# Decays folded into the queries of the linear attention, and the softmax attention's query preparation written behind its scores

## The chip, the cores and the metric

One NeuronCore of a Trainium2 chip runs the whole block as one program. The metric is the device time of one launch in microseconds (us), as the median of three runs. Matrix work is done by TensorE (PE in the profile; its weight loads are listed apart as PEld), elementwise work by VectorE (DVE) and ScalarE (ACT), a little by GpSimd (POOL). Transfers are issued by SyncE (SP).

## The reference

One encoder block over 1024 tokens of width 1024, all in float32. Two branches read the same normalised input; only what the change touches is spelled out here.

```
h = RMSNorm(x);  [linear q,k,v,r, gate codes, softmax q,k,v, branch gates] = h @ W_in
# linear attention, 4 heads, keys of 128, values of 256, forward and backward:
#   S_t = exp(log_g_t) * S_{t-1} + k_t v_t^T,   o_t = q_t^T S_t
q_dec = q * exp(b); k_inv = k * exp(-b)                 # b: running sum of log_g in a chunk
o = tril(q_dec k_inv^T) v  +  q_dec @ state             # state of the chunks before
state = exp(b_last) * state + k_tail^T v
# softmax attention, 8 query heads on 2 key heads, blocks of 128, window +-128, sink:
p = softmax([scores of three neighbouring key blocks, sink]);  o = p v
x = x + (sigmoid(gA) * (A @ W_a) + sigmoid(gB) * (B @ W_b)) @ W_out
x = x + SwiGLU(RMSNorm(x))
```

The decay `exp(b_last)` is one number for each key channel. It multiplies the state by rows, and the query meets the state along the same channels; so the decay may as well multiply the query.

## The kernel before, in words

Large products are computed as three matmuls on split operands: each float32 tensor becomes a rounded high part (ACT copies it to fp32r) and a low part (DVE subtracts). `wunit` (lines 66 to 73) loads a weight tile, splits it on ACT (line 70) and DVE (line 72), and the dense projections use it.

The program runs in stages: projections to DRAM scratch (to about 330 us), linear attention (about 330 to 545 us), softmax attention (about 545 to 735 us), output projections and the feed-forward part (to the end). In the two attention stages the dense projections that are still due fill TensorE: `slot(stages, n)` (line 206) calls the stage functions of one step in a given order and lets n matmuls of dense work run, spread evenly between them. TensorE takes its instructions in just this written order (`manual_schedule`). The other engines' queues are ordered by a list scheduler which prefers what is written earlier among what its model takes to be ready; so moving a function in the source moves its instructions on ACT, DVE and SP, and may move others too.

Linear attention works on 32 chunks of 128 tokens (4 heads by 8), two chunks (a pair) at a time for the gates. `g_gates` (625) computes the running sums `cs` and their small summary `sm`; `g_powers` (662) makes the powers, and from them `en` (keys) and `q2` (queries, forward and backward); `g_scores` (683) transposes keys and makes the masked scores; `g_out` (708) makes the key-value products `kv` of a chunk, carries the forward state `pf` and adds query times state to the output `o`; `g_back` (735) and `g_back_out` (747) do the same backwards with `kb`, `o2`; `g_turn` (767) transposes the output. In `g_out` ACT makes the decay `dec` (a [128,1] exponential, line 719), then the decayed state `th` (721), which TensorE multiplies by the queries; DVE makes the next state (722). `g_back` does likewise with `decb` (741), `thb` (743) and line 745. `k_norm` (780) normalises and rotates the softmax attention's keys, written at the stage's end, and the scheduler lets it float forward.

Softmax attention works on 16 steps (2 key heads by 8 blocks; 4 query heads at a time). `a_prep` (905) normalises and rotates queries on ACT (866) and DVE (912 to 917); `a_turn` (919) transposes them; `a_scores` (931) makes the scores of four heads, each in a PSUM bank, which DVE masks, copies out and reduces to a maximum (line 941); after the fourth, DVE makes the negative maximum `nm` (948 to 950), ACT takes four exponentials (956), DVE adds up (`dn`, 958) and inverts, GpSimd scales (962). `a_probs` (964) transposes probabilities two steps later, ACT and DVE split them (976, 977), and `a_out` (980) multiplies them with the values; ACT copies the result out (`sob`, 987). All these small products share four PSUM banks (`chtile`, line 49), while dense work has four of its own. Within a step the functions are sorted by the tuple `order`:

```
order = (a_probs, k_prep, a_prep, a_scores, a_turn, k_turn, a_out, k_load, a_load)
```

Of the kernel before, what the change touches and what calls it, by code (L numbers as in the profile page):

```python
# [11 lines left out]
AF = mybir.ActivationFunctionType  # L12
ALU = mybir.AluOpType

P = 128
# [15 lines left out]
def body(tc, i, out):  # L31
    nc = tc.nc
    with ExitStack() as root:
# [8 lines left out]
        def nm(s):  # L42
            uid[0] += 1
            return f"{s}_{uid[0]}"
# [4 lines left out]
        def chtile(shape, dt=F32):  # L49
            return psc.tile(list(shape), dt, tag="ch", name=nm("ch"))  # L50
# [24 lines left out]
        def mm(o, a, b, start, stop):  # L75
            nc.tensor.matmul(o, a, b, start=start, stop=stop)  # L76

        def mm3(o, ah, al, bh, bl, start, stop):
            mm(o, ah, bh, start, False)
            mm(o, ah, bl, False, False)  # L80
            mm(o, al, bh, False, stop)
# [459 lines left out]
        with tc.manual_schedule(engines={mybir.EngineType.PE}):  # L541
# [8 lines left out]
            for k in range(KT):  # L550
# [5 lines left out]
                c = slice((k % 4) * P, (k % 4 + 1) * P)  # L556
# [63 lines left out]
        def gtile(tag, shape=(P, 256), dt=F32, bufs=2):  # L620
            return gt.tile(list(shape), dt, tag=tag, name=nm(tag), bufs=bufs)

        gla = {}
# [38 lines left out]
        def g_powers(hd, c):  # L662

            pr = gla[hd, c].pr
            qk, e, cs = pr.qk, pr.e, pr.cs
            ef, csf = (v.rearrange("p d j t -> p (d j t)") for v in (e, cs))
            nc.vector.tensor_tensor(e[:, 0], cs[:, 0], cs[:, 0, :, 63:64].to_broadcast([P, 2, P]), op=ALU.subtract)
            nc.vector.tensor_tensor(e[:, 1, :, 1:P], cs[:, 1, :, 0:P - 1], cs[:, 1, :, 63:64].to_broadcast([P, 2, P - 1]),
                                    op=ALU.subtract)
            nc.vector.tensor_scalar(e[:, 1, :, 0:1], cs[:, 1, :, 63:64], -1.0, None, op0=ALU.mult)  # L670

            x1 = cs.rearrange("p d j t -> p d (j t)")
            x2 = e.rearrange("p d j t -> p d (j t)")
            nc.scalar.activation(csf, ef, AF.Exp, scale=-1.0 / 16)
            nc.scalar.activation(ef, ef, AF.Exp, scale=1.0 / 16)
            pr.en = gtile("en", (P, 2, 256))
            nc.vector.tensor_tensor(pr.en[:, 0], x2[:, 0], qk[:, 1], op=ALU.mult)
            nc.vector.tensor_tensor(pr.en[:, 1], x1[:, 1], qk[:, 1], op=ALU.mult)
            pr.q2 = (gtile("q2f", bufs=3), gtile(f"q2b{c}", bufs=(3, 2, 2, 1)[c // 2]))
            nc.vector.tensor_tensor(pr.q2[0], x1[:, 0], qk[:, 0], op=ALU.mult)  # L680
            nc.vector.tensor_tensor(pr.q2[1], x2[:, 1], qk[:, 0], op=ALU.mult)
# [26 lines left out]
        def g_out(hd, c):  # L708

            a = gla[hd, c]  # L710
            kv = chtile((P, 2, 256))
            for d in range(2):
                mm3(kv[:, d], a.kth[:, d], a.ktl[:, d], a.vh, a.vl, True, True)
            a.pf = gtile("pf")
            if c:
                pf = gla[hd, c - 1].pf
                dec = gtile("dec", (P, 1))
                p = gla[hd, c - 1]
                nc.scalar.activation(dec, a.pr.sm[:, 0, a.j, 0:1], AF.Exp, bias=p.pr.sm[:, 0, p.j, 1:2])
                th = gtile("th")  # L720
                nc.scalar.activation(th, pf, AF.Copy, scale=dec[:, 0:1])
                nc.vector.scalar_tensor_tensor(a.pf, pf, dec[:, 0:1], kv[:, 0], op0=ALU.mult, op1=ALU.add)
                a.kb = gtile(f"kb{c}", bufs=2 if c < 5 else 1)
                nc.scalar.copy(a.kb, kv[:, 1])
            else:
                nc.vector.tensor_copy(a.pf, kv[:, 0])
                a.kb = None
            o = chtile((P, 256))
            mm3(o, a.sh, a.sl, a.vh, a.vl, True, c == 0)
            if c:  # L730
                mm(o, a.pr.q2[0][:, a.t], th, False, True)
            a.ob = gtile(f"ob{c}", bufs=2 if c < 5 else 1)
            nc.scalar.copy(a.ob, o)

        def g_back(hd, c):

            a = gla[hd, c]
            if c < NC - 1:
                n = gla[hd, c + 1]
                dec = gtile("decb", (P, 1))  # L740
                nc.scalar.activation(dec, a.pr.sm[:, 1, a.j, 1:2], AF.Exp, bias=n.pr.sm[:, 1, n.j, 0:1])
                a.thb = gtile("thb")
                nc.scalar.activation(a.thb, n.kb, AF.Copy, scale=dec[:, 0:1])
                if c:
                    nc.vector.scalar_tensor_tensor(a.kb, n.kb, dec[:, 0:1], a.kb, op0=ALU.mult, op1=ALU.add)

        def g_back_out(hd, c):
            a = gla[hd, c]
            if c < NC - 1:
                o2 = chtile((P, 256))  # L750
                mm(o2, a.pr.q2[1][:, a.t], a.thb, True, True)
                nc.vector.tensor_tensor(a.ob, a.ob, o2, op=ALU.add)
            if c:
                g_back(hd, c - 1)

            if c % 2:
                a.ss = gtile("oss", (P, 2))
            ss = a.ss if c % 2 else gla[hd, c + 1].ss
            sq = gtile("osq", bufs=1)
            nc.scalar.activation(sq, a.ob, AF.Square, accum_out=ss[:, 1 - c % 2:2 - c % 2])  # L760
            if c % 2 == 0:
                rs = gtile("ors", (P, 2))
                rsqrt(rs, ss, 1.0 / 256, EPS, epst, gt, (P, 2), "on")
                for j, v in enumerate((gla[hd, c + 1].ob, a.ob)):
                    nc.scalar.activation(v, v, AF.Copy, scale=rs[:, j:j + 1])
# [41 lines left out]
        for n in range(NH * NC):  # L807
            hd, c = divmod(n, NC)
# [11 lines left out]
        with tc.manual_schedule(engines={mybir.EngineType.PE}):  # L820
            fill(24)
            for t in range(last + 1):
                n = 24 if t < 2 else 16 if t < 4 else 12 if t < NH * NC + 4 else 8 if t < last - 1 else 18
# [56 lines left out]
        def k_load(t):  # L880
            raws[t] = sw.tile([P, 256], F32, tag="kvr", name=nm("kvr"))
            need(("skv", t))
            nc.sync.dma_start(out=raws[t], in_=scr["skv", t][:, 256:512])
            keys[t] = sw.tile([P, 2, P], F32, tag="key", name=nm("key"))
            nc.sync.dma_start(out=keys[t].rearrange("p a b -> p (a b)"), in_=scr["key", t])
# [127 lines left out]
        for n in range(2 * KT):  # L1013
# [9 lines left out]
                if n:  # L1023
                    todo[n - 1].append((k_load, n))
            todo[n].append((a_load, g, t))
        order = (a_probs, k_prep, a_prep, a_scores, a_turn, k_turn, a_out, k_load, a_load)
        k_load(0)
        with tc.manual_schedule(engines={mybir.EngineType.PE}):
            for t, v in enumerate(todo):
# [507 lines left out]
```

## Time and profile before

| | |
|---|---|
| median of 3 runs | 1645.83 us (1645.22 to 1646.64) |
| the profiled execution | 1645.61 us, its span 1643.8 us |
| PE busy in the span | 1626.0 us, 99% |
| DVE, ACT, POOL busy | 1251.4, 842.6, 76.0 us |
| granted TensorE clock | 1.000 |
| transfers | 262.91 MB, 160 GB/s on average |

The profile is one execution; its rows of time (windows, waits, groups of equal instructions, timeline) count microseconds from the span's start. An engine's busy time holds the instructions themselves and not their waiting; matmuls overlap in their records, so PE looks busy as long as it is fed. A row of waits names who waited, at which line, for whom, the total, how often and the longest.

### The profile page before, as it was taken

Reading aid. Unit: us, or ns where it says so; the run is one execution under the profiler, and the core shown is the slowest. Engines: PE = TensorE matmul, PEld = TensorE weight load, DVE = VectorE, ACT = ScalarE, POOL = GpSimd, SP = SyncE. Lnnn points to the kernel's source line nnn. Section 1 sums busy time; section 2 is a strip of 40 time slices with the busy share of each in tenths; the row PEclk is TensorE's granted clock in tenths of the full one; section 3 lists DMA queues with packets and bytes.
Section 4 is the critical chain, followed back from the end, with each engine's and each line's share of the span. In section 5 each row is a group of like instructions: output and inputs, shape, how many; then the busy total and the mean of one; then the engine's idle time right before and its main releaser. Section 6 shows DMA issues by size and latency. Waiting matters only on the chain.

```text
span 1643.8 us, 23281 instructions
## 1 busy us (share of the span) xinstructions
PE 1626.0 (99%) x7588; PEld 1346.0 (82%) x7588; DVE 1251.4 (76%) x2559; ACT 842.6 (51%) x1762; POOL 76.0 (5%) x68
## 2 busy tenths in 40 slices
PE   9999999999999989999999999999999999999999
PEld 7888888888888778888888888888888888888887
DVE  8866665589986598867885678887777778779655
ACT  8622224468998666665554557333333333354442
POOL 0000000000000034540000000000000000000000
PEclk9999999999999999999999999999999999999999
DMA  7554334475554633248765544443334443596433
GB/s 238 176 178 148 115 122 135 173 250 173 179 161 129 191 108 97 77 138 280 225 205 175 168 146 145 140 149 109 109 115 147 142 147 129 177 341 193 149 98 119
DMA packets 168010, 262.91 MB, mean 160 GB/s; under 512 B 19324, under 2 KB 52860, under 8 KB 167888
## 3 DMA queue, kind: packets, MB, share of 16 engines
q1 hardware_dynamic: 167888, 261.42, 49.8%
q8 instruction: 60, 0.98, 0.2%
q14 instruction: 62, 0.51, 0.1%
HBM read 187.93 MB, written 73.42 MB: 159 GB/s over the span
## 4 chain that ended last, share of the span: by engine, by line
PE 84%; DVE 9%; ACT 4%; DMA 2%; issue 1%; POOL 1%; SPq 0%; ACTq 0%; DVEq 0%
PE mm L76 23%; PE mm L306 9%; PE mm L308 9%; PE mm L307 9%; PE mm L1350 7%; PE ch L1350 5%; PE ch L76 4%; PE ch L306 4%; PE ch L308 4%; PE ch L307 4%; PE ch L460 3%; PE mm L460 2%; ACT p L956 1%; DVE wl L72 1%; DVE cs L655 1%
## 5 line engine op out<-in xcount | busy, mean ns | idle before, releaser
L298 ACT ACTIVATE wh<-ws 128x512 fp32r<-128x512 f32 x132 | 83.3, 632 | 195.9 <-PE mm L307 102.2
L70 ACT ACTIVATE wh<-wr 128x512 fp32r<-128x512 f32 x202 | 124.9, 626 | 87.4 <-PE mm L76 54.9
L72 DVE TENSOR_TENSOR wl<-wr,wh 128x512 fp32r<-128x512 f32 x202 | 137.7, 686 | 26.8 <-ACT wh L70 26.4
L299 DVE TENSOR_TENSOR wl<-ws,wh 128x512 fp32r<-128x512 f32 x132 | 90.5, 686 | 22.7 <-ACT wh L298 22.6
L298 ACT ACTIVATE wh<-wr 128x512 fp32r<-128x512 f32 x69 | 43.6, 632 | 124.8 <-issue 49.7
L962 POOL TENSOR_SCALAR p<-p,rd 128x384 f32<-128x384 f32 (+1 forms) x64 | 75.8, 1202 | 657.1 <-DMA qr<-sq 587.2
L298 ACT ACTIVATE wh<-a 128x512 fp32r<-128x512 f32 x64 | 40.5, 633 | 91.4 <-PE ch L1350 42.3
L76 PE MATMUL mm<-wh,xl 128*128 128x512 f32 x192 | 83.1, 433 | 0.0
L76 PE MATMUL mm<-wh,xh 128*128 128x512 f32 x192 | 79.6, 415 | 0.0
L76 PE MATMUL mm<-wl,xh 128*128 128x512 f32 x192 | 79.6, 414 | 0.0
L299 DVE TENSOR_TENSOR wl<-a,wh 128x512 fp32r<-128x512 f32 x64 | 44.2, 691 | 43.1 <-ACT wh L298 42.5
L1350 PE MATMUL mm<-hh,wh 128*128 128x512 f32 x176 | 68.5, 389 | 0.0
L1350 PE MATMUL mm<-hl,wh 128*128 128x512 f32 x176 | 68.5, 389 | 0.0
L1350 PE MATMUL mm<-hh,wl 128*128 128x512 f32 x176 | 68.5, 389 | 0.0
L76 PE MATMUL mm<-xl,wh 128*128 128x512 f32 x160 | 64.5, 403 | 0.1
L76 PE MATMUL mm<-xh,wh 128*128 128x512 f32 x160 | 64.4, 403 | 0.2 <-ACT wh L70 0.2
L76 PE MATMUL mm<-xh,wl 128*128 128x512 f32 x160 | 59.2, 409 | 0.0
L1320 DVE TENSOR_TENSOR hl<-hr,hh 128x512 fp32r<-128x512 f32 x75 | 51.4, 685 | 3.7 <-ACT hh L1319 3.7
L1350 PE MATMUL ch<-hh,wh 128*128 128x512 f32 x132 | 51.3, 389 | 0.0
L1350 PE MATMUL ch<-hl,wh 128*128 128x512 f32 x132 | 51.3, 389 | 0.0
L1350 PE MATMUL ch<-hh,wl 128*128 128x512 f32 x132 | 51.3, 389 | 0.0
L76 PE MATMUL mm<-oah,wh 128*128 128x512 f32 x128 | 50.2, 392 | 0.0
(620 smaller groups left out, 5077.7 us busy)
## 6 DMA issues: line engine op xcount, KB each, us to landing
wr<-in_w_fi_dram SPq DMA_DIRECT2D x102, 256.0 KB
wr<-in_w_f_dram SPq DMA_DIRECT2D x80, 256.0 KB
wr<-in_w_t_dram SPq DMA_DIRECT2D x56, 256.0 KB
B<-c SPq DMA_DIRECT2D x44, 256.0 KB
T<-tx SPq DMA_DIRECT2D x44, 256.0 KB
a<-in_w_fo_dram SPq DMA_DIRECT2D x44, 256.0 KB
hr<-T SPq DMA_DIRECT2D x44, 256.0 KB
wr<-in_w_ob_dram SPq DMA_DIRECT2D x32, 256.0 KB
```

What stands on the lines that cost most here:

```text
L70: nc.scalar.activation(h, raw, AF.Copy)
L72: nc.vector.tensor_tensor(l, raw, h.bitcast(F32), op=ALU.subtract)
L76: nc.tensor.matmul(o, a, b, start=start, stop=stop)
L298: nc.scalar.activation(h, src, AF.Copy)
L299: nc.vector.tensor_tensor(l, src, h.bitcast(F32), op=ALU.subtract)
L306: nc.tensor.matmul(o, h[:, c], x[kk][0], start=start and kk == 0, stop=False, skip_group_check=True)
L307: nc.tensor.matmul(o, h[:, c], x[kk][1], start=False, stop=False, skip_group_check=True)
L308: nc.tensor.matmul(o, l[:, c], x[kk][0], start=False, stop=kk == nk - 1, skip_group_check=True)
L460: nc.tensor.matmul(ys[m], a[:, c], b, start=f0, stop=f1, skip_group_check=True)
L962: nc.gpsimd.tensor_scalar(p[:, h, :w], p[:, h, :w], rd[:, h:h + 1], None, op0=ALU.mult)
L1320: nc.vector.tensor_tensor(l, r, h.bitcast(F32), op=ALU.subtract)
L1350: nc.tensor.matmul(ys[m], a[:, c], b, start=f0, stop=f1, skip_group_check=True)
```

## The change

Two edits. First, in the linear attention, all decays of a pair of chunks are made at once: DVE adds the two log decays for each chunk boundary into a small tile `dec` ([128, 2, 2]), and ACT takes one exponential of it for the pair. The decay then multiplies the 128x128 slice of queries in place on DVE, and TensorE multiplies these queries by the undecayed state (`pf`, or the next chunk's `kb`). ACT no longer makes `th` and `thb`. The state updates on DVE stay, with the new decay as their scalar. Second, in the softmax attention, `a_scores` stands ahead of `k_prep` and `a_prep` in the step's order.

```diff
@@ g_powers
+            pr.dec = gtile("dec", (P, 2, 2), bufs=16)
+            nc.vector.tensor_tensor(pr.dec[:, 1], pr.sm[:, :, 1, 0], pr.sm[:, :, 0, 1], op=ALU.add)
+            if c:
+                nc.vector.tensor_tensor(pr.dec[:, 0], pr.sm[:, :, 0, 0], gla[hd, c - 1].pr.sm[:, :, 1, 1], op=ALU.add)
+            dc = pr.dec[:, 0 if c else 1:2]
+            nc.scalar.activation(dc, dc, AF.Exp)
@@ g_out
-                dec = gtile("dec", (P, 1))
-                p = gla[hd, c - 1]
-                nc.scalar.activation(dec, a.pr.sm[:, 0, a.j, 0:1], AF.Exp, bias=p.pr.sm[:, 0, p.j, 1:2])
-                th = gtile("th")
-                nc.scalar.activation(th, pf, AF.Copy, scale=dec[:, 0:1])
-                nc.vector.scalar_tensor_tensor(a.pf, pf, dec[:, 0:1], kv[:, 0], op0=ALU.mult, op1=ALU.add)
+                dec = a.pr.dec[:, a.j, 0:1]
+                q = a.pr.q2[0][:, a.t]
+                nc.vector.tensor_scalar(q, q, dec, None, op0=ALU.mult)
+                nc.vector.scalar_tensor_tensor(a.pf, pf, dec, kv[:, 0], op0=ALU.mult, op1=ALU.add)
...
-                mm(o, a.pr.q2[0][:, a.t], th, False, True)
+                mm(o, q, pf, False, True)
@@ g_back
-                dec = gtile("decb", (P, 1))
-                nc.scalar.activation(dec, a.pr.sm[:, 1, a.j, 1:2], AF.Exp, bias=n.pr.sm[:, 1, n.j, 0:1])
-                a.thb = gtile("thb")
-                nc.scalar.activation(a.thb, n.kb, AF.Copy, scale=dec[:, 0:1])
+                dec = (n if a.j else a).pr.dec[:, 1 - a.j, 1:2]
+                q = a.pr.q2[1][:, a.t]
+                nc.vector.tensor_scalar(q, q, dec, None, op0=ALU.mult)
+                a.after = n.kb
                 if c:
-                    nc.vector.scalar_tensor_tensor(a.kb, n.kb, dec[:, 0:1], a.kb, op0=ALU.mult, op1=ALU.add)
+                    nc.vector.scalar_tensor_tensor(a.kb, n.kb, dec, a.kb, op0=ALU.mult, op1=ALU.add)
@@ g_back_out
-                mm(o2, a.pr.q2[1][:, a.t], a.thb, True, True)
+                mm(o2, a.pr.q2[1][:, a.t], a.after, True, True)
@@
-        order = (a_probs, k_prep, a_prep, a_scores, a_turn, k_turn, a_out, k_load, a_load)
+        order = (a_probs, a_scores, k_prep, a_prep, a_turn, k_turn, a_out, k_load, a_load)
```

The numbers of instructions that change: ACT loses 28 `th`, 28 `thb` and 56 single decays and gains 16 exponentials of a pair; DVE gains 28 small additions and 56 multiplications of a query slice. TensorE has the same matmuls as before, in nearly the same places.

What this does to the engines' queues is seen at three places. The first is ACT in the linear attention, in the step after the transposed output of an earlier head, about the chunk whose state update is `pf_4541` before. `kb` and `ob` are the copies that free the two PSUM banks of `g_out`, `osq`, `oss` and `rl` belong to the output's normalisation, `kth` is the next chunk's split keys. Before:

```order
L741 ACTIVATE decb_4902<-sm_4026,sm_4197 128x1
L760 ACTIVATE osq_4519,oss_4406<-ob_751_3586 128x256
L98 ACTIVATE rl_4522<-oss_4406,eps 128x2
L99 ACTIVATE rl_4522<-rl_4522 128x2
L724 COPY kb_1055_4547<-ch_4534 128x256
L733 COPY ob_1057_4554<-ch_4549 128x256
L721 ACTIVATE th_4630<-pf_4541,dec_4628 128x256
L695 ACTIVATE kth_4565<-ch_4562 128x256
```

In the changed kernel the same place reads (its line numbers are 5 to 7 higher here, and `st` is dense work's output, `ob` with `ors` the normalisation's last step):

```order
L765 ACTIVATE osq_4501,oss_4391<-ob_750_3591 128x256
L98 ACTIVATE rl_4504<-oss_4391,eps 128x2
L99 ACTIVATE rl_4504<-rl_4504 128x2
L729 COPY kb_1028_4526<-ch_4516 128x256
L738 COPY ob_1030_4533<-ch_4528 128x256
L186 ACTIVATE st_4559<-mm_3976,rstdt 128x512
L770 ACTIVATE ob_771_3665<-ob_771_3665,ors_4503 128x256
L770 ACTIVATE ob_750_3591<-ob_750_3591,ors_4503 128x256
L702 ACTIVATE kth_4544<-ch_4541 128x256
```

The decayed state and the single decay are gone from between the bank-freeing copies, and other work stands closer behind them.

The second place is DVE in the second step of the softmax attention's scores. `dn` and `rd` belong to the first step's softmax, `st` and `wl` to dense work, `rt` to the queries' normalisation. Before, the four rows of line 941, which free the score banks, begin here:

```order
L914 TENSOR_TENSOR sq_7173<-qr_7166,qB 128x4x64
L125 TENSOR_TENSOR st_7193<-mm_6983,rstd 128x512
L917 TENSOR_TENSOR qn_7186<-qn_7186,sq_7173 128x512
L958 TENSOR_TENSOR dn_7130<-dn_7130,es_7127 128x4
L102 TENSOR_TENSOR rt_7181<-rt_7181,rl_7178 128x4
L125 TENSOR_TENSOR st_7197<-mm_6984,rstd 128x512
L960 RECIPROCAL rd_7136<-dn_7130 128x4
L103 SCALAR_TENSOR_TENSOR rt_7181<-rt_7181,rl_7178 128x4
L72 TENSOR_TENSOR wl_7206<-wr_7202,wh_7204 128x512
L104 SCALAR_TENSOR_TENSOR rs_7177<-rt_7181,rl_7178 128x4
L941 ISA p_7209,mx_7210<-ch_7211,band 128x384
```

In the changed kernel the rows of the same step (line 946 there) come like this:

```order
L932 TENSOR_TENSOR sql_7042<-ch_7036,sqh_7041 128x512
L908 TENSOR_TENSOR kTl<-ch_7046,kTh 128x2x128
L72 TENSOR_TENSOR wl_7090<-wr_7086,wh_7088 128x512
L946 ISA p_7062,mx_7063<-ch_7064,band 128x384
L946 ISA mx_7063 128x1
L125 TENSOR_TENSOR st_7077<-mm_6875,rstd 128x512
L963 TENSOR_TENSOR dn_6999<-dn_6999,es_6996 128x4
L946 ISA p_7062,mx_7063<-ch_7070,band 128x384
L946 ISA mx_7063 128x1
L965 RECIPROCAL rd_7005<-dn_6999 128x4
L125 TENSOR_TENSOR st_7081<-mm_6876,rstd 128x512
L946 ISA p_7062,mx_7063<-ch_7093,band 128x384
```

The first bank-freeing row has moved ahead of the first step's sum `dn` and of the dense work's two outputs, and the queries' preparation is no longer before it.

The third place is ACT in a middle step of the softmax attention. `sqh` splits the turned queries, `sob` copies the output of `a_out`, lines 956 and 961 are the exponentials, `ph` splits the turned probabilities of the next step. Before:

```order
L926 ACTIVATE sqh_7945<-ch_7940 128x512
L987 COPY sob_7961<-ch_7951 128x512
L953 ACTIVATE es_7924<-es_7924 128x4
L956 ACTIVATE p_7894,dn_7927<-p_7894,nm_7920,rs_7591 128x384 x4
L976 ACTIVATE ph_7977<-ch_7972 128x512
```

The same step in the changed kernel:

```order
L931 ACTIVATE sqh_7837<-ch_7832 128x512
L961 ACTIVATE p_7767,dn_7800<-p_7767,nm_7793,rs_7545 128x384
L958 ACTIVATE es_7797<-es_7797 128x4
L961 ACTIVATE p_7767,dn_7800<-p_7767,nm_7793,rs_7545 128x384 x3
L992 COPY sob_7853<-ch_7843 128x512
L981 ACTIVATE ph_7869<-ch_7864 128x512
```

The copy of the output has moved from ahead of the exponentials to behind them. It stands ahead of them in 10 of the 16 steps before and in 5 of the 16 in the changed kernel.

## The prediction

> **What bounds the kernel now.** I read the page's busy times first, then the table of windows by stage, then the waits of TensorE's weight loads in the two attention stages, and last the timeline at the places found.
>
> ```profile
> span 1643.8 us, 23281 instructions
> PE 1626.0 (99%) x7588; PEld 1346.0 (82%) x7588; DVE 1251.4 (76%) x2559; ACT 842.6 (51%) x1762; POOL 76.0 (5%) x68
> ```
>
> TensorE is busy in 99% of the span, so the total is its work plus 17.8 us of idleness. No change here removes TensorE work; what can be won is waiting. The windows (columns: stretch, its length, busy time and instructions of PE, PEld, DVE, ACT, POOL, then clock and transfers) say where that is. The first three are the linear attention, the next two the softmax attention.
>
> ```profile
> 345.00:385.00 40.00, 40.00 (x235) 34.85 (x234) 37.13 (x124) 31.15 (x81) 0.00 (x0) 1.00 0.67 204
> 385.00:465.00 80.00, 78.56 (x456) 66.00 (x455) 77.65 (x283) 73.62 (x225) 0.00 (x0) 1.00 0.57 174
> 465.00:545.00 80.00, 79.00 (x443) 66.58 (x442) 55.94 (x172) 70.67 (x215) 0.00 (x0) 1.00 0.47 141
> 545.00:605.00 60.00, 55.24 (x274) 44.68 (x272) 43.55 (x137) 36.74 (x99) 9.06 (x8) 1.00 0.54 165
> 605.00:735.00 130.00, 125.22 (x680) 105.36 (x681) 107.65 (x353) 86.17 (x227) 66.76 (x56) 1.00 0.31 98
> 735.00:1643.00 908.00, 905.09 (x3992) 748.15 (x3990) 692.49 (x1108) 392.18 (x661) 0.00 (x0) 1.00 0.51 165
> ```
>
> From 735 us on TensorE is busy 905.09 of 908.00 us, so a microsecond won earlier arrives at the end nearly whole. In the linear attention ACT is busy 92% from 385 to 465 us and DVE 97%, and TensorE begins to miss. In the softmax attention TensorE loses 4.76 and 4.78 us while no engine is full: there chains of latency decide. PE's idle time understates the loss, since the records of matmuls overlap; a weight load that stands still says it better. Its waits from 345 to 545 us:
>
> ```profile
> PEld ch L76 <- ACT ob L733: 3.5, 6, 0.9
> PEld ch L771 <- ACT ob L765: 1.3, 2, 0.9
> PEld ch L771 <- DVE ktl L696: 1.3, 2, 0.7
> PEld ch L76 <- DVE ktl L696: 1.3, 4, 0.5
> PEld ch L76 <- ACT kb L724: 1.1, 3, 0.5
> ```
>
> 5.9 us of waiting are ACT's (3.5 + 1.3 + 1.1), 2.6 us DVE's; 8.5 us together. From 545 to 735 us the longest are these, the last two rows being PE's own:
>
> ```profile
> PEld ch L76 <- DVE mx L941: 4.4, 5, 0.9
> PEld ch L923 <- DVE mx L941: 2.5, 2, 2.3
> PEld ch L76 <- DVE pl L977: 2.5, 4, 1.0
> PEld ch L973 <- POOL p L962: 1.8, 3, 0.8
> ...
> PE ch L923 <- DVE mx L941: 1.9, 1, 1.9
> PE ch L973 <- POOL p L962: 0.9, 2, 0.6
> ```
>
> Three of the four weight-load rows wait for DVE to free a bank of scores (941) or of turned probabilities (977).
>
> **The decays: what ACT loses.** The groups from 345 to 545 us:
>
> ```profile
> L721 ACT ACTIVATE th<-pf,dec 128x256 f32<-128x256 f32 x28 | 14.5, 518 | 0.2
> L743 ACT ACTIVATE thb<-kb,decb 128x256 f32<-128x256 f32 x28 | 14.1, 511 | 1.1 <-PE ch L76 1.1
> ...
> L741 ACT ACTIVATE decb<-sm 128x1 f32<-128x1 f32 x16 | 4.6, 286 | 0.8 <-DVE sm L660 0.7
> L719 ACT ACTIVATE dec<-sm 128x1 f32<-128x1 f32 x15 | 4.6, 304 | 0.0
> ```
>
> 14.5 and 14.1 us go with the decayed states. The 56 single exponentials go at between 0.286 and 0.304, say 0.295 us: 16.5 us. Sixteen exponentials of four numbers or fewer come back at the same price, 4.7 us. ACT is relieved of 14.5 + 14.1 + 16.5 - 4.7 = 40.4 us over 200 us, that is 16.2 us in an 80 us window: 73.62 falls to about 57, or 72%. At 345 to 385 us ACT was busy 31.15 of 40.00, 78%, and TensorE idle for nothing. So I expect most of ACT's 5.9 us of waits to go and take seven tenths: 4.1 us. Bounds: nothing, and all 5.9.
>
> **What DVE gains.** The prices come from these groups of the same window:
>
> ```profile
> L72 DVE TENSOR_TENSOR wl<-wr,wh 128x512 fp32r<-128x512 f32 x38 | 26.0, 687 | 5.0 <-ACT wh L70 5.0
> ...
> L705 DVE CAST sh<-sp 128x128 fp32r<-128x128 f32 x32 | 7.1, 223 | 0.2
> L650 DVE TENSOR_SCALAR e<-e 128x512 f32<-128x512 f32 x15 | 6.3, 423 | 0.4 <-ACT e L648 0.4
> L793 DVE SCALAR_TENSOR_TENSOR qn<-kvr,rs,kg 128x128 f32<-128x128 f32 x16 | 5.4, 348 | 0.2
> ...
> L659 DVE TENSOR_SCALAR sm<-cs 128x8 f32<-128x8 f32 x15 | 2.5, 166 | 0.0
> ```
>
> No row shows a 128x128 multiplication by a column of scalars. From below: 423 ns for 512 and 166 ns for 8 elements make 0.51 ns an element, so 166 + 61 = 227 ns for 128, near the cast's 223. From above: the operation with two tensors and such a scalar, 348 ns. I take 250, close to the cast, since it too has one source: 56 x 0.25 = 14.0 us (12.5 to 19.5). The 28 additions at the 128x8 row's 166 ns are 4.6 us. DVE gains 18.6 us (17.1 to 24.1), and its 170.7 us (37.13 + 77.65 + 55.94) become 189.3 of 200, or 95%. That was about its share at 345 to 385 us (37.13 of 40.00), where TensorE did not wait. In the queue the additional work stands where its data have long been there: the queries were last read by the scores two steps earlier, the decay by the pair's powers. Behind a multiplication stands the state's update, which waits for `kv` anyway. So the price is that `ktl` and the bank-freeing copies come a little later; I let DVE's 2.6 us of waits grow by half, 1.3 us. Linear attention: -4.1 + 1.3 = -2.8 us.
>
> A rule of the Trainium skill bears on the first price. Row L72, with two tensors, takes 687 ns for 512 elements, row L650, with one, 423. "VectorE: DVE Perf Modes", in the section on mode 2x_2P, says that a float32 operation with a single SBUF source streams two elements a cycle, and one with two tensors one, which these two rows agree with. Its 0.96 GHz would make 67 ns of the 128 elements, an estimate from that page, and the 56 multiplications about 12.5 us instead of 14.0.
>
> **The order of the scores.** TensorE's work is the same, with the dense matmuls around the scores shifted by two or three. What changes is when DVE frees score banks. At the stage's start:
>
> ```profile
> 586.24 0.16 DVE L958 TENSOR_TENSOR dn<-dn,es 128x4 f32<-128x4 f32 x1
> 587.98 0.55 DVE L941 CUSTOM_DVE_ANT_0 p<-ch,band 128x384 f32<-128x384 f32 x1
> 588.60 0.66 PE L923 MATMUL ch<-ident,qn 128*128 128x128 f32 x4 [1.86 <-DVE mx L941]
> ```
>
> The second step's first score bank was read at 587.98 us, 1.7 us after `dn`, and TensorE's transposes had stood for 1.86 us. In the changed queue that read stands ahead of `dn`, and the other three are only two larger rows behind it. So this 1.9 us should go, and with the earlier maximum the exponentials and GpSimd's scaling come earlier, for which the turned probabilities of the first two steps waited 0.9 us. I take 2.5 of these 2.8 us (bounds 0 and 2.8), since the next wait, for `sqh` or a bank of `pl`, is near.
>
> In the middle of the stage two effects oppose each other. ACT's queue there:
>
> ```profile
> 641.83 0.17 DVE L950 TENSOR_SCALAR nm<-mx 128x4 f32<-128x4 f32 x1
> 642.35 0.59 ACT L987 COPY sob<-ch 128x512 f32<-128x512 f32 x1 [1.96 <-PE ch L76]
> 642.94 0.70 ACT L956 ACTIVATE p<-p,nm,rs 128x384 f32<-128x384 f32 x1
> ACT sob L987 <- PE ch L76: 16.9, 10, 2.0
> ```
>
> The negative maximum was ready at 642.00 and the exponentials began at 642.94, for ACT held the output's copy ahead of them, which waited for TensorE. Five of the ten such places go: up to 0.94 us each, 4.7 us. But then the copy's 0.59 us lies behind the exponentials and ahead of `ph`, and the next scores' first bank waits for it: 5 x 0.59 = 3.0 us. Also DVE reads the first score bank behind three `pl` rather than ahead of them in several steps. I count zero here, with 3 us to either side.
>
> **The sum.** The profiled execution took 1645.61 us, 0.2 under the median. 1645.6 - 2.8 - 2.5 + 0 = **1640.3 us**.
>
> **Rivals.** *DVE becomes the bound, and it is slower.* From 385 to 465 us DVE was busy 77.65 of 80.00. At the upper price it gains 24.1 / 200 x 80 = 9.6 us there: 87.3 us, 7.3 over. If nothing can be deferred TensorE waits for that, and with the softmax stage's 2.5 us won the time is 1645.6 + 7.3 - 2.5 = 1650.4. It decides once DVE's undeferrable work in such a stretch exceeds the stretch. For it speaks the 97%; against it, that the keys' normalisation (line 793 is a part of it) is filler here, and the window after has 24 us free. The Trainium skill speaks for this rival: "Perfetto Trace Analysis", in Optimizing Scalar/DVE Operations, advises to move work from a saturated DVE to ScalarE, and this edit moves it the other way. By that rule the time would be the 1650.4; the row at 345 to 385 us, 93% busy with TensorE at 40.00 of 40.00, does not bear it out. Chance 0.09.
>
> *The chain through the softmax steps gets longer.* The copy behind the exponentials costs its 3.0 us and saves nothing, as the steps are held by `pl` and line 941 (7 us of weight-load waits). Then 1645.6 - 2.8 - 2.5 + 3.0 = 1643.3, no change. Equally, new waits may take the place of those at the stage's start. Chance 0.22.
>
> *All waits named go.* 5.9 us of ACT's without DVE's price, 2.8 at the start, and in the middle 4.7 less 1.7, a little over half of the copy's 3.0: 1645.6 - 5.9 - 2.8 - 3.0 = 1633.9. Chance 0.14.
>
> **How the numbers follow.** The forecast has the remaining 0.55; its own range, from its bounds, is 1637 to 1643. 0.2% is 3.3 us, about what a measurement of this kernel tells from no change, so faster means under 1642.5 and slower over 1649.1. Of the forecast's 0.55 some 0.04 lies over 1642.5. Faster: 0.51 + 0.14 + 0.02 of the second rival = 0.67. Slower: 0.09 of the first, with 0.01 for what is not named, 0.10. The same: 0.23. The range that holds 8 in 10 reaches from 1634.5, most of the way to the third rival, to 1646.5, past the second.
>
> **What would show it.** Right, if after the change ACT is busy near 57 us of 80 from 385 to 465 us and the rows of waits for `ob` and `kb` shrink below 2 us together, while DVE grows by 17 to 24 us over the stage and `ktl` is waited for 3 to 5 us; if the transposes at about 588 us wait under 0.5 us for line 941's successor; if `sob` is waited for about half as often. Each step has its own row: a multiplication of queries far over 0.35 us breaks the DVE term, waits of weight loads on the multiplied queries or `pf` break the claim that they are early, and more than 8 us of waits on DVE or ACT between 605 and 735 us break the zero. The prediction is wrong as a whole if TensorE's waits in the linear attention stay above 7 us, or the softmax stage is not shorter.

## The result and the profile after

The changed kernel takes 1642.28 us (median of 15 runs, 1641.54 to 1643.32), the kernel before in the same rounds 1645.42 (15 runs, 1643.94 to 1646.64). The ratio is 0.9982, 95% interval 0.9975 to 0.9989: 3.1 us or 0.19% less, a real gain that lies just at the 0.2% named as the limit, 0.2 us on the near side of 1642.5. The forecast of 1640.3 lies 2.0 us below the measured time. The profiled execution took 1642.09 us, with a span of 1640.3, 3.5 us shorter than before.

First the page's busy times of the changed kernel.

```profile
span 1640.3 us, 23265 instructions
PE 1626.2 (99%) x7588; PEld 1345.8 (82%) x7588; DVE 1259.8 (77%) x2643; ACT 813.8 (50%) x1666; POOL 75.5 (5%) x68
```

TensorE's work is the same. ACT lost 28.8 us and DVE gained 8.4, where the forecast had 40.4 and 18.6. The windows by stage, columns as before:

```profile
345.00:385.00 40.00, 40.00 (x235) 34.95 (x234) 38.17 (x138) 26.65 (x68) 0.00 (x0) 1.00 0.65 198
385.00:465.00 80.00, 78.63 (x455) 65.99 (x455) 78.42 (x295) 60.85 (x180) 0.00 (x0) 1.00 0.55 169
465.00:545.00 80.00, 78.99 (x443) 66.23 (x442) 63.77 (x227) 59.76 (x177) 0.00 (x0) 1.00 0.48 147
545.00:605.00 60.00, 57.10 (x284) 46.38 (x283) 44.51 (x140) 37.00 (x100) 11.68 (x11) 1.00 0.53 163
605.00:735.00 130.00, 127.11 (x693) 106.23 (x692) 109.03 (x358) 88.15 (x229) 63.62 (x54) 1.00 0.34 105
```

The edits show up in quite different places. In the linear attention (the first three rows) ACT's busy time fell from 175.44 to 147.26 us, and TensorE's went from 197.56 to 197.62: nothing was won there. In the softmax attention TensorE is busy 1.86 us more in 545 to 605 us and 1.89 us more in 605 to 735. That is 3.75 us, enough for the whole of the shorter span.

The waits of TensorE's weight loads from 345 to 545 us in the changed kernel:

```profile
PEld ch L76 <- ACT kb L729: 3.0, 6, 0.9
PEld ch L76 <- PE mm L76: 1.4, 3, 0.6
PEld ch L76 <- DVE ob L757: 0.9, 1, 0.9
PEld ch L776 <- DVE ktl L703: 0.8, 2, 0.5
...
PEld ch L76 <- ACT ob L738: 0.5, 1, 0.5
```

With the rows left out they come to 8.8 us, against 8.5 before. The wait for `ob` went, from 3.5 (line 733) to 0.5 (738), but the wait for the other copy of the same step, `kb`, grew from 1.1 to 3.0, and the rest are waits on other things. From 545 to 735 us:

```profile
PEld ch L76 <- DVE mx L946: 4.0, 6, 1.0
PEld ch L76 <- DVE pl L982: 3.5, 7, 0.7
PEld ch L76 <- DVE kTl L908: 2.3, 3, 1.1
PEld ch L76 <- ACT sob L992: 1.8, 4, 0.6
PEld ch L928 <- DVE qn L922: 1.4, 1, 1.4
...
PEld ch L978 <- POOL p L967: 0.2, 1, 0.2
```

The waits of transposes for a score bank (2.5 us before) are gone, those for GpSimd's scaling fell from 1.8 to 0.2, while those for `pl`, `kTl` and `sob` grew.

### The profile page after: what moved, and what is told of

It reads as the page before. It is cut to its first block, busy times and chain, and to the rows that moved or that the text cites. A ratio compares the mean times of both kernels' runs of the same rounds, so it can differ in the third digit from the quotient of the medians.

```text
span 1640.3 us, 23265 instructions
## 1 busy us (share of the span) xinstructions
PE 1626.2 (99%) x7588; PEld 1345.8 (82%) x7588; DVE 1259.8 (77%) x2643; ACT 813.8 (50%) x1666; POOL 75.5 (5%) x68
## 4 chain that ended last, share of the span: by engine, by line
PE 84%; DVE 11%; ACT 3%; DMA 1%; issue 1%; SPq 0%; ACTq 0%; DVEq 0%
PE mm L76 23%; PE mm L306 9%; PE mm L308 9%; PE mm L307 9%; PE mm L1355 7%; PE ch L1355 5%; PE ch L76 4%; PE ch L306 4%; PE ch L308 4%; PE ch L307 4%; PE ch L460 3%; PE mm L460 2%; DVE wl L72 1%; DVE cs L655 1%; ACT p L961 1%
```

## The experiments

The theory after the result: the whole gain is the order's; in the linear attention DVE became the limit, so ACT's relief was spent on waiting for DVE. The rival is the forecast's own split. All ratios are against the kernel before, in the same rounds.

**The decays alone.**

```diff
 (the changed kernel)
-        order = (a_probs, a_scores, k_prep, a_prep, a_turn, k_turn, a_out, k_load, a_load)
+        order = (a_probs, k_prep, a_prep, a_scores, a_turn, k_turn, a_out, k_load, a_load)
```

> The changed kernel with the order line as it was before: the decays multiply the queries, but the queries' preparation again stands ahead of the scores. Theory: in linear attention ScalarE's gain is spent on waiting for VectorE, so this part is worth nothing: 1645.4 us +-1 (the time of the kernel before), with TensorE's weight-load waits between 345 and 545 us near 8.8 us as in the changed kernel and 8.5 in the kernel before. Rival, the prediction's own term: this part brings -2.8 us, 1642.6 us. Second rival: VectorE's extra 8 us cost more than they hide, 1647 us or more.

Measured: 1645.75 us against 1645.42, ratio 1.0004 (0.9994 to 1.0013). The edit in the linear attention is worth nothing that shows; the interval, -1.0 to +2.1 us, leaves out the forecast's -2.8.

**The order alone.**

```diff
 (the kernel before)
-        order = (a_probs, k_prep, a_prep, a_scores, a_turn, k_turn, a_out, k_load, a_load)
+        order = (a_probs, a_scores, k_prep, a_prep, a_turn, k_turn, a_out, k_load, a_load)
```

> The kernel before with the new order line alone: the decays multiply the states as before. Theory: all of the change's -3.1 us comes from the order, so 1642.3 us +-1, with the 1.9 us stall of the transposes near 588 us gone and TensorE's busy time between 545 and 605 us up from 55.24 to about 57. Rival, the prediction's sizes turned round: the order brings -0.5 us or less and the rest came from the decays, 1645 us.

Measured: 1641.37 us, ratio 0.9976 (0.9967 to 0.9985), that is -4.0 us by the medians, against -3.1 for both edits together. Its windows of the softmax attention:

```profile
545.00:605.00 60.00, 57.77 (x287) 46.95 (x286) 45.11 (x142) 36.96 (x101) 12.27 (x11) 1.00 0.52 164
605.00:735.00 130.00, 127.09 (x692) 106.23 (x691) 108.88 (x354) 88.93 (x230) 63.04 (x54) 1.00 0.34 106
```

TensorE gains 2.53 us in the first and 1.87 in the second. The order alone gives all of the gain. Whether it gives more than both edits together is not settled, since the two intervals overlap.

**The multiplications on GpSimd, and on ScalarE.**

```diff
 (the changed kernel, in g_out and g_back)
-                nc.vector.tensor_scalar(q, q, dec, None, op0=ALU.mult)
+                nc.gpsimd.tensor_scalar(q, q, dec, None, op0=ALU.mult)
```

> The changed kernel with the 56 query multiplications moved from VectorE, where they take 278 ns each and 15.6 us in all, to GpSimd, which does nothing between 345 and 545 us. Theory: VectorE is what linear attention waits for, directly or through ScalarE's waits for it, so 15.6 us less on it give 2 to 4 us: 1638.3 to 1640.3 us, with the waits on the key copy, the outputs and the key remainders together down from 8.8 us to 5 or less. Rival: VectorE is not the limit and what is left are chains through TensorE's own banks: within 1 us of 1642.3. Second rival: GpSimd takes so long for one multiplication, or contends with VectorE, that the products of queries and states wait for it: 1644 us or more.

```diff
 (the changed kernel, in g_out and g_back)
-                nc.vector.tensor_scalar(q, q, dec, None, op0=ALU.mult)
+                nc.scalar.activation(q, q, AF.Copy, scale=dec)
```

> The changed kernel with the 56 query multiplications moved from VectorE to ScalarE, as scaled copies; at 280 to 300 ns each this takes 15.6 us from VectorE and puts 16 to 17 us back on ScalarE, which has 60.85 busy of 80 us between 385 and 465 us against VectorE's 78.42. Theory, VectorE limits: 1 to 3 us less than the changed kernel, 1639.3 to 1641.3 us. Rival, it is ScalarE's load and chain that counts as in the kernel before: 1642.3 to 1645 us.

Measured: on GpSimd 1644.55 us, ratio 0.9994 (0.9985 to 1.0003); on ScalarE 1641.95, ratio 0.9981 (0.9971 to 0.9990), where the changed kernel has 1642.28 and 0.9982. GpSimd's row for the forward queries in the first run, from 345 to 545 us:

```profile
L726 POOL TENSOR_SCALAR q2f<-q2f,dec 128x128 f32<-128x128 f32 x28 | 28.7, 1023 | 110.0 <-PE ch L76 106.6 <-DVE pf L727 3.3
```

GpSimd takes 1.02 us for one of these in place of 0.28, and 0.79 us for one of the backward queries. The time is that of the second rival. Its mechanism is not shown: no weight load waits for GpSimd by name, while those for `ktl` come to 4.2 us in place of 0.8 and those for `ob` of line 738 to 2.1 in place of 0.5. ScalarE takes 0.41 us, and relieving DVE with it brought nothing that can be told from zero. The theory that DVE is the limit had failed twice, but each of these runs moved a load to another place. The next two change it in place.

**Without the multiplications.**

```diff
 (the changed kernel, in g_out and g_back)
-                nc.vector.tensor_scalar(q, q, dec, None, op0=ALU.mult)
 (in g_back_out)
-            nc.scalar.activation(sq, a.ob, AF.Square, accum_out=ss[:, 1 - c % 2:2 - c % 2])
+            nc.scalar.activation(sq, a.ob, AF.Square, scale=1e-4, accum_out=ss[:, 1 - c % 2:2 - c % 2])
```

> The changed kernel without its 56 query multiplications: the products take the undecayed queries, and a constant scale of 1e-4 in the outputs' squares keeps their sums in range, so the outputs lack the decay. ScalarE keeps the whole relief of the change and VectorE is spared 56 x 278 ns = 15.6 us. This splits the forecast's two terms for linear attention. The forecast's sizes: -4.1 us from ScalarE's relief is there and VectorE's price, forecast at 1.3 us, was in truth about 4: then 1638 to 1639.5 us, with the weight-load waits from 345 to 545 us down from 8.8 to 4 or 5. Rival: ScalarE's relief itself is worth nothing, because its copies wait for VectorE or TensorE whatever ScalarE's load is: 1641.3 to 1642.3 us, waits still 7 us or more.

Measured: 1641.80 us, ratio 0.9977 (0.9968 to 0.9986). This is no faster than the order alone (1641.37, 0.9976), though ACT has all of its relief and DVE hardly more work than before. Its windows of the linear attention:

```profile
385.00:465.00 80.00, 78.83 (x454) 65.63 (x453) 76.70 (x284) 61.87 (x183) 0.00 (x0) 1.00 0.57 169
465.00:545.00 80.00, 79.43 (x448) 67.01 (x447) 57.78 (x192) 59.57 (x172) 0.00 (x0) 1.00 0.48 146
```

The rival holds, with 8.3 us of weight-load waits in the linear attention: ScalarE's relief is worth nothing that shows by itself, even where DVE carries hardly more. The forecast's 4.1 us for it would have put this run below the order alone, at about 1637, and its interval begins at 1640.4. ACT has more than 11 us less work in each of these windows than before (73.62 and 70.67), DVE no more in the first and 1.8 us more in the second, and TensorE has won 0.27 and 0.43 us.

**The multiplications twice.**

```diff
 (the changed kernel, in g_out and g_back)
                 nc.vector.tensor_scalar(q, q, dec, None, op0=ALU.mult)
+                nc.vector.tensor_scalar(q, q, dec, None, op0=ALU.mult)
```

> The changed kernel with each query multiplication made twice in place, so that the queries are decayed twice: 15.6 us more on VectorE in linear attention and nothing else. If VectorE's load is what sets linear attention there: 2 to 4 us more, 1644.3 to 1646.3 us, with longer waits for VectorE and for ScalarE's copies behind it. Rival, load moves little as long as the order allows deferring: within 0.7 us of 1642.3.

Measured: 1643.59 us, ratio 0.9987 (0.9978 to 0.9997), 1.3 us more than the changed kernel, between the two expectations. DVE's load does cost something, but little: with no multiplications and with two, in the same rounds, the time is 1641.80 and 1643.59. The changed kernel's 1642.28 comes from other rounds, so the shares of the first and the second multiplication are not resolved.

**The new order in the first six steps only.**

```diff
 (the kernel before)
         order = (a_probs, k_prep, a_prep, a_scores, a_turn, k_turn, a_out, k_load, a_load)
+        early = (a_probs, a_scores, k_prep, a_prep, a_turn, k_turn, a_out, k_load, a_load)
...
-                v.sort(key=lambda e: order.index(e[0]))
+                v.sort(key=lambda e: (early if t < 6 else order).index(e[0]))
```

> The kernel before with the new order in the first six steps of the softmax attention only; from the seventh on the old one, so the copies of the output stand ahead of the exponentials as before. The forecast: the start is worth -2.5 us and the middle nothing, so 1642.9 us, and nearly all of what the order alone gave (-4.0). By the windows of the run with the order alone: -2.5 in 545 to 605 us and -1.9 in 605 to 735, so also 1642.9 us and 1.5 us more than the order alone. Rival, the gain sits in the middle steps: 1644 us or more. Second rival, it is all at the start: 1641.4 us.

Measured: 1644.26 us against 1645.68, ratio 0.9991 (0.9982 to 1.0000), that is -1.4 us. Its windows:

```profile
545.00:605.00 60.00, 57.58 (x286) 46.81 (x286) 44.55 (x140) 37.31 (x101) 11.70 (x11) 1.00 0.53 164
605.00:735.00 130.00, 125.19 (x681) 104.84 (x680) 108.02 (x354) 87.64 (x227) 64.33 (x54) 1.00 0.32 101
```

The first window has nearly the gain of the order alone (2.34 of 2.53 us), the second none (125.22 before). So by the windows the two parts add up as those of the order alone said. The time does not agree as well: it lies above the 1642.9 that the forecast and the windows gave, and in the rival's range. Part of the difference lies outside the softmax attention: from 385 to 545 us, whose code this edit does not touch, TensorE is busy 157.24 us in this execution and 157.56 before. The interval, 0 to -3.0 us, allows either reading; the middle steps are worth 1.9 us by the windows and 2.6 us by the medians.

**The queries' preparation alone behind the scores.**

```diff
 (the kernel before)
-        order = (a_probs, k_prep, a_prep, a_scores, a_turn, k_turn, a_out, k_load, a_load)
+        order = (a_probs, k_prep, a_scores, a_prep, a_turn, k_turn, a_out, k_load, a_load)
```

> The kernel before with only the queries' preparation moved behind the scores; the values' split stays ahead of them. Theory: the queries' preparation (four VectorE rows of 512 elements and a normalisation) is what stood ahead of the score banks, so all of the order's gain: 1641.4 to 1642 us. Rival, the values' split on ScalarE and VectorE in the first eight steps counts as well: 1643 us or more.

Measured: 1642.49 us against 1645.68, ratio 0.9981 (0.9972 to 0.9990), that is -3.2 us, between the two expectations. TensorE is busy 127.07 us from 605 to 735, as with the whole order, and 56.13 from 545 to 605, about a third of the way from 55.24 to 57.77. By the windows the queries' preparation carries all of the middle; the values' split, `k_prep`, seems to carry a part of the start, about 0.8 us, which the medians' intervals don't settle.

**The key state's copy first.** The theory by now: what holds the linear attention is the places at which the queues of ACT and DVE stand behind one another, not how full they are.

```diff
 (the changed kernel, in g_out)
-                nc.vector.tensor_scalar(q, q, dec, None, op0=ALU.mult)
-                nc.vector.scalar_tensor_tensor(a.pf, pf, dec, kv[:, 0], op0=ALU.mult, op1=ALU.add)
                 a.kb = gtile(f"kb{c}", bufs=2 if c < 5 else 1)
                 nc.scalar.copy(a.kb, kv[:, 1])
+                nc.vector.scalar_tensor_tensor(a.pf, pf, dec, kv[:, 0], op0=ALU.mult, op1=ALU.add)
+                nc.vector.tensor_scalar(q, q, dec, None, op0=ALU.mult)
```

> The changed kernel with the key state's copy written ahead of the forward state's update and of the query multiplication in each chunk; the work is the same. In the changed kernel ScalarE stands 9.0 us between 345 and 545 us at this copy for VectorE's update, which reads the same bank, and TensorE's weight loads then stand 3.0 us for the copy. Theory now, after the run without multiplications: neither engine's load holds linear attention, but the places at which their queues wait for each other. Then those 9.0 us go, TensorE's waits for the copy fall below 1 us, and the time falls by 1 to 2.5: 1639.8 to 1641.3 us. Rival: the wait moves to the update and to TensorE's next bank, within 0.6 us of 1642.1.

Measured: 1640.44 us (6 runs, 1640.13 to 1640.92) against 1645.77, ratio 0.9969 (0.9958 to 0.9981). All of its runs lie below all of the changed kernel's (from 1641.54), and below all of the next run's (from 1641.66), which were made in the same rounds: 1.8 us less than the changed kernel, by the medians, for the same work in another order. It is the fastest kernel of the study. Its windows and its weight loads' waits in the linear attention:

```profile
385.00:465.00 80.00, 79.01 (x463) 67.19 (x462) 78.36 (x294) 60.70 (x183) 0.00 (x0) 1.00 0.54 169
465.00:545.00 80.00, 79.44 (x442) 66.19 (x441) 64.26 (x233) 59.59 (x178) 0.00 (x0) 1.00 0.48 148
```

```profile
PEld ch L76 <- DVE pf L728: 1.8, 4, 0.5
...
PEld ch L76 <- ACT ob L738: 0.4, 2, 0.2
```

DVE and ACT are as full as in the changed kernel, and TensorE is busy 0.83 us more over these two windows. By itself that proves little, since the next run has 0.76 us more and no gain. A better mark is the end of the stage, as TensorE's order is fixed: from the first products with `kth` to the last transposes of `ob` it takes 202.1 us here, 203.5 in the changed kernel, 203.0 in the next run, and 203.2 to 203.8 in the four kernels that have the linear attention of before and no other move. So most of the gain lies in this stage: 1.4 us, where the span is 1.6 us shorter than the changed kernel's. No weight load waits for `kb` any more (3.0 us); 1.8 us for `pf` have come in its place, since the update now stands behind the copy. ACT's own waits for DVE have hardly shrunk, 40.2 us in all against 41.7: those of `kb` are gone, and those of `cs` for the pair's decay (line 673) grew from 2.6 to 12.4 us. The edit also puts the update ahead of the multiplication; which of its two moves pays was not separated.

**The squares one step later, and both moves.** Here `g_norm` holds the squares and what follows them, taken out of `g_back_out`.

```diff
 (the changed kernel)
+        def g_norm(hd, c):
+            a = gla[hd, c]
             if c % 2:
                 a.ss = gtile("oss", (P, 2))
...
+            at[cb + 1, 8] = (g_norm, hd, c)
...
-                slot([(lambda v=at[t, j]: v[0](*v[1:])) if (t, j) in at else None for j in (0, 6, 5, 4, 3, 2, 1, 7)], n)
+                slot([(lambda v=at[t, j]: v[0](*v[1:])) if (t, j) in at else None for j in (0, 6, 8, 5, 4, 3, 2, 1, 7)], n)
```

> The changed kernel with the squares of an output (and what follows of its normalisation) written one step later; the work is the same. In the changed kernel ScalarE stands 10.7 us at these squares for VectorE's addition, ahead of the copies that free banks. Theory (queues that wait for each other): these waits go, and the time falls by 1 to 2.5 us: 1639.6 to 1641.1 us. Rival: the output's normalisation then comes late for its transposes, or the waits move to the exponentials of the powers: 1641.5 us or more.

> The changed kernel with both moves, the key state's copy ahead of the update and the squares one step later. Theory: ScalarE's waits for VectorE between 345 and 545 us fall from about 40 us by some 20, TensorE's weight-load waits from 8.8 to 5 us or less, and the time to 1638 to 1640 us, below the order alone (1641.4). Rival: waits move on, TensorE's weight-load waits stay above 7 us and the time within 0.8 us of 1642.1.

The last run is the order alone with the same two moves.

> The new order alone (decays on the states, as before) with both moves. If ScalarE's relief pays once its queue no longer stands behind VectorE, this one, without the relief, stays 1.5 us or more above the changed kernel with both moves: 1640.5 us or more. Rival: the moves do without the relief all they can do, or nothing, and the order alone with them is as fast or faster: at or below the changed kernel with both moves.

Measured: the squares later 1642.34 us, ratio 0.9981 (0.9972 to 0.9990); both 1642.95, 0.9982 (0.9973 to 0.9991); the order alone with both 1642.64, 0.9981 (0.9973 to 0.9990). All three expectations of the theory failed. The squares' wait did not go: ACT's row of waits in the first of the three has 13.3 us of it, more than the changed kernel's 10.7.

```profile
ACT osq L767 <- DVE ob L757: 13.3, 16, 1.5
```

In ACT's queue the squares still come where they must wait for that addition, so this edit did not do what it was meant to and does not test the theory. With both moves the waits for `ob` come back (2.2 us) and the gain of the copy's move is lost; why these two moves disturb each other is not settled. The last run, without ACT's relief, takes the same time as the one before it within what can be told, so no worth of the relief shows in this order either. The fastest kernel without the relief, that is the order alone with the copy's move, was not run; whether the relief pays there stays open.

## Why the prediction was right and wrong

The time came out within the forecast's own range of 1637 to 1643, but as the sum of one term that was too large and one that was too small, so the agreement is luck. Linear attention was to give -2.8 and gave +0.3 when tried alone (-1.0 to +2.1); the softmax attention was to give -2.5 and its order alone gave -4.0 (-5.4 to -2.5). The prediction called itself wrong as a whole if TensorE's waits in the linear attention stayed above 7 us: they are 8.8. Its other signs for that stage failed too: `ob` and `kb` are waited for 3.5 us in the rows shown, not under 2, and DVE grew by 9.6 us, not 17 to 24. The signs for the softmax attention held, though the one set for its middle (8 us of waits, where there are 7.6) did not catch that the zero was off.

**The step that failed: "So I expect most of ACT's 5.9 us of waits to go".** It went from shares of busy time to waits: ACT was to be 72% busy, and at 78% TensorE had not waited. The relief itself was over-counted, 40.4 us by rows against 28.2 in the windows, and ACT is busy 60.85 of 80 us where about 57 was forecast. But size was not the trouble, since in the run without the multiplications even the whole relief, with 1.4 us added on DVE, buys no time that shows. The timeline of the kernel before, ACT only, shows what a share can't. At 439.18 us TensorE's weight load has waited 0.79 us for the copy `ob`:

```profile
436.99 1.16 ACT L70 ACTIVATE wh<-wr 128x512 fp32r<-128x512 f32 x2
438.03 0.42 ACT L760 ACTIVATE osq<-ob 128x256 f32<-128x256 f32 x1
...
438.57 0.30 ACT L98 ACTIVATE rl<-oss,eps 128x2 f32<-128x2 f32 x1
438.78 0.35 ACT L733 COPY ob<-ch 128x256 f32<-128x256 f32 x1
```

TensorE's last products into a bank of `ob` are this row:

```profile
436.64 0.60 PE L76 MATMUL ch<-th,q2f 128*128 128x256 f32 x2
```

They were done by 437.24, and the copy began 1.5 us later. What stood ahead of it was dense work's split, the squares and a logarithm, and no decayed state. The same place in the changed kernel, where the wait is 0.55 us and for `kb`, one row earlier in the queue:

```profile
436.39 1.18 ACT L70 ACTIVATE wh<-wr 128x512 fp32r<-128x512 f32 x2
437.43 0.44 ACT L765 ACTIVATE osq<-ob 128x256 f32<-128x256 f32 x1
...
438.00 0.29 ACT L98 ACTIVATE rl<-oss,eps 128x2 f32<-128x2 f32 x1
438.32 0.20 ACT L99 ACTIVATE rl<-rl 128x2 f32<-128x2 f32 x1
438.43 0.35 ACT L729 COPY kb<-ch 128x256 f32<-128x256 f32 x1
438.68 0.38 ACT L738 COPY ob<-ch 128x256 f32<-128x256 f32 x1
```

The removed work was not in the way here: the splits, the squares and the logarithm still stand ahead of the copies. With the key state's copy written first they stand there too, but the squares come between the two splits and 1.1 us earlier, the copies follow 0.9 to 1.0 us earlier, and the wait is 0.22 us:

```profile
436.33 0.43 ACT L765 ACTIVATE osq<-ob 128x256 f32<-128x256 f32 x1
...
436.73 0.64 ACT L70 ACTIVATE wh<-wr 128x512 fp32r<-128x512 f32 x1
...
437.44 0.38 ACT L727 COPY kb<-ch 128x256 f32<-128x256 f32 x1
...
437.79 0.39 ACT L738 COPY ob<-ch 128x256 f32<-128x256 f32 x1
```

One place is not all of them. The forecast's 5.9 us are eleven waits of weight loads for ACT. In seven of them, 3.9 us, none of the removed rows stands in ACT's queue between its last idle time (over 0.05 us) and the row that is waited for; in the other four (403, 415, 450 and 462 us), 2.1 us, some do. So about half of the 4.1 us that were forecast could go by shorter work at all. In the changed kernel the rows of waits for ACT come to 4.2 us, 1.7 less, while those for DVE and for TensorE's own products grew from 2.6 to 4.6. And in four of its six waits for `kb` ACT had stood idle for 1.3 to 1.6 us at the squares, ahead of the copy, for DVE's addition. These are the squares ahead of the copy that is waited for at 427.10 us before and at 426.65 after:

```profile
425.71 0.42 ACT L760 ACTIVATE osq<-ob 128x256 f32<-128x256 f32 x1 [0.23 <-DVE ob L752]
```

```profile
425.10 0.42 ACT L765 ACTIVATE osq<-ob 128x256 f32<-128x256 f32 x1 [1.57 <-DVE ob L757]
```

Where the freed time went is seen in ACT's own longest waits from 345 to 545 us, before and after:

```profile
ACT cs L674 <- DVE e L670: 9.3, 10, 2.1
ACT kb L724 <- DVE pf L722: 6.1, 14, 1.0
...
ACT osq L760 <- DVE ob L752: 1.6, 4, 0.8
```

```profile
ACT cs L681 <- DVE e L670: 11.9, 9, 2.6
ACT osq L765 <- DVE ob L757: 10.7, 14, 1.6
ACT kb L729 <- DVE pf L727: 9.0, 15, 1.4
```

These three grew from 17.0 to 31.6 us, and all of ACT's waits for DVE from 19.5 to 41.7: most of the 28.2 us became standing behind DVE, with the copies behind them in the queue. An engine with less work in the same stretch must idle more, so these rows say whom ACT waited for and not what that cost. That the order can cost this stage time with the loads unchanged is shown by the one move that won 1.8 us. That order is what holds the stage at every place isn't shown: the other move did not take its wait away, and the two together won nothing.

**DVE's price** can't be told from the 1.3 us that had been set. Two errors in it go opposite ways: one multiplication takes 278 ns, not 250, but rows of DVE overlap, and 19.7 us of additional rows fill only 9.6 us of the windows (170.72 to 180.36). The multiplications cost 0.5 us by the medians of the changed kernel and of the run without them, a difference below what those intervals resolve. `ktl` is waited for 0.8 us in the row shown, less than the 3 to 5 forecast.

**The softmax stage's start** held. The transposes that had stood for 1.86 us at 588.60 have no wait in the changed kernel, and the waits for GpSimd fell by 1.6 us. By the windows the start is worth 2.3 to 2.5 us with the decays as before, against 2.5 forecast; the medians of the run with the early steps alone say 1.4, with an interval that reaches from 0 to 3.0. In the changed kernel it is 1.9: the first transposes of queries there wait 0.98 us for `qn`, 0.26 in the run with the order alone, so the fuller DVE seems to hand the stage over later.

**The softmax stage's middle** was mis-sized: zero was forecast, and it is worth 1.9 us by the windows (2.6 by medians). The copy `sob` is waited for by ACT at 5 places in place of 10, as forecast:

```profile
ACT sob L992 <- PE ch L76: 7.3, 5, 2.0
```

Its price behind the exponentials, 3.0 us in the sum, was set too high: from 605 to 735 us TensorE's weight loads wait 0.5 us for `sob` before and 1.2 after. In the same stretch all of their waits fell from 9.8 to 7.6 us, which fits the 1.9. The score banks went from 4.4 to 4.0, `pl` stayed (2.5 and 2.4; its growth lies in the stage's start), GpSimd's 0.4 went, and so did 2.0 us in front of score products that no other engine is named for. Which of these the copy's move saved is not shown; what the runs show is that the order in the middle steps, and the queries' preparation in it, makes the gain.

**The rivals.** "DVE becomes the bound" is ruled out: DVE is at 78.42 of 80 us, yet the kernels with no and with two multiplications lie only 1.8 us apart, where 7.3 had been set. The Trainium skill says in "Perfetto Trace Analysis", Optimizing Scalar/DVE Operations, that moving work from a saturated DVE to ScalarE may make sense. It was tried: 1641.95 against 1642.28 us, which can't be told from no change. "The chain through the softmax steps gets longer" is nearest in time (1643.3, nearer than the forecast), but the chain got shorter. "All waits named go" failed with the linear attention.

## What to carry to other kernels

An engine's share of busy time does not say what a wait on it is made of: before taking work off an engine, look in the timeline at the instructions that stood in its queue ahead of the one waited for, and count only what is removed from between them. Work that is removed from elsewhere in the queue can turn into waiting for the next engine, as most of it did here. In this kernel, writing a copy ahead of an update that reads the same bank, and moving preparations behind the step that frees banks, were worth 1.8 and 4.0 us, while 28 us of work taken off one engine won nothing that could be measured in the orders compared.

## What the hardware showed that was not expected

Rows of the profile overlap on DVE. The changed kernel's queue there:

```profile
399.79 0.28 DVE L726 TENSOR_SCALAR q2f<-q2f,dec 128x128 f32<-128x128 f32 x1
399.99 0.48 DVE L750 SCALAR_TENSOR_TENSOR kb<-kb,dec,kb 128x256 f32<-128x256 f32 x1
400.38 0.42 DVE L685 TENSOR_TENSOR en<-cs,qk 128x256 f32<-128x256 f32 x1
```

A multiplication of 0.28 us holds up the next instruction for 0.20. So a sum of mean durations, as the prediction made it, overstates what an instruction adds to a busy queue. The Trainium skill says so in "Perfetto Trace Analysis", Optimizing Scalar/DVE Operations: of an instruction's data-access latency the write-acknowledgement half overlaps with the next instruction. This trace agrees in that rows overlap, here by 0.08 us.

The multiplication by a column of scalars takes as long as an operation with two tensors. The groups of the changed kernel:

```profile
L713 DVE TENSOR_TENSOR sl<-sp,sh 128x128 fp32r<-128x128 f32 x32 | 9.1, 284 | 0.1
L726 DVE TENSOR_SCALAR q2f<-q2f,dec 128x128 f32<-128x128 f32 x28 | 7.8, 278 | 0.7 <-PE ch L76 0.7
L712 DVE CAST sh<-sp 128x128 fp32r<-128x128 f32 x32 | 7.0, 219 | 0.1
```

278 ns is near the 284 of two tensors, not the 219 of the cast. The Trainium skill's "VectorE: DVE Perf Modes", in the section on mode 2x_2P, grants two elements a cycle to float32 operations with one tensor and a scalar; for a scalar from a column this trace does not bear that out, and the measured 278 ns decides. With one size measured, a lower rate and a longer fixed part can't be told apart.

On ACT an exponential of four numbers without a bias column takes 200 ns, where the single ones before, with a bias column, took 286 to 304; the prediction had set the same price for both.
